# Issuing the later adaLN rows from ScalarE's queue in a one-core transformer layer

## The chip, the core and the metric

One core of a Trainium2 chip runs one transformer layer from HBM to HBM in one launch. The metric is the device time in microseconds of that launch. The engines are named as in the profile: PE is TensorE (matrix products), DVE is VectorE, ACT is ScalarE, POOL is GpSimd, and SP is the sync engine, which here issues transfers and nothing else. Every engine works through its own list of instructions in order; an instruction whose input is not there holds all that stand behind it on the same engine.

## The reference

SEQ is 256 tokens, D is 2048, the feed-forward width is 5632:

```python
ada = silu(c) @ w_ada + b_ada                     # 2048 -> 9 x 2048
sh1, sc1, g1, sh2, sc2, g2, sh3, sc3, g3 = split(ada, 9)
h = _swiglu(_modulate(x, sh1, sc1), ffn1_w_in, ffn1_w_out)
x = _layernorm(ALPHA * x + 0.5 * (1 + g1) * h, ln1_g, ln1_b)
h = _token_mixer(_modulate(x, sh2, sc2), w_in, ...)    # Fox attention and an mLSTM, side by side
x = _layernorm(ALPHA * x + (1 + g2) * h, ln2_g, ln2_b)
h = _swiglu(_modulate(x, sh3, sc3), ffn2_w_in, ffn2_w_out)
x = _layernorm(ALPHA * x + 0.5 * (1 + g3) * h, ln3_g, ln3_b)

def _modulate(x, shift, scale): return _layernorm(x) * (1 + scale) + shift
def _swiglu(h, w_in, w_out):
    gate, up = split(h @ w_in, 2)
    return (silu(gate) * up) @ w_out
```

All of it is float32. The vector `silu(c) @ w_ada` is the part that this case is about: one row vector times a matrix of 2048 x 18432, 151 MB, of which each number is used once.

## The kernel before

**Weights.** Each large product is made of three matrix products of rounded halves: a weight is split into `hi` (rounded to fp32r) and `lo = raw - hi`, and `mm3` multiplies hi by hi, hi by lo and lo by hi (lines L445 to L447; `mm2`, L450 and L451, is a form of it with two instructions). `load_w` brings a weight tile of 1 MB into one of three `raw` buffers (transfer issued by SP, L406), and `split` makes two halves of it: ScalarE casts `hi` (`S.copy`, L155) and VectorE subtracts `lo` (L156). There are six `hi` and six `lo` buffers. In most stages one half tile feeds twelve matmuls of 512 columns. Names: `raw_f1i9_11` is the raw tile of the first FFN's input weights, group 9, tile 11; `hi_f1i9_110` and `lo_f1i9_110` are its first half, `..._111` its second. `fv512` are columns of the mixer's input weights that make the Fox values; there a raw tile is cut in four, `hi_fv512_10` to `hi_fv512_13`.

**Ada rows.** VectorE computes `silu(c) @ w_ada` while TensorE multiplies weights. A *unit* is 1024 columns of `w_ada`; its 2048 input rows come as sixteen tiles of 128 x 1024, "rows" in this text, 512 KB each. `ask` takes the next row from the list `wanted`, takes one of two `araw` buffers, and issues its transfer (L192); `ada_acc` scales each of the 128 partitions by its element of `silu(c)` and adds it to the unit's accumulator (L168 for the first row, L170 for the others: `acc <- ar, csil, acc`). In `ada_rows` each accumulation is followed by the request for the next row, so one row is under way while another is used, and the row two later can only be issued when the accumulation of this one has ended. `ar3_0_14` is row 14 of unit 3_0. When a unit is complete, `pair_tail` or `gate_tail` split the sum and add it over the partitions on TensorE (`alo`, `bc`).

**What sets the order.** `AdaQueue` paces the rows: `pump(n)` and `half_step()` let about 1.1 to 1.3 rows through per raw weight tile, and `pinned()` places a row's work behind the newest weight cast; `need(n)` forces units to be complete ahead of their use. Within that, a scheduler that works from its own estimates puts the instructions of each engine in a fixed list when the kernel is built. The first rows, until about 220 us, are issued by GpSimd (L955); 224 later ones by `ask`. SP's list is thus a mixture of weight tiles (L406) and rows (L192).

Of the kernel before, what the change touches and what calls it, by code (L numbers as in the profile page):

```python
# [14 lines left out]
P = 128  # L15
# [17 lines left out]
def layer_kernel(  # L33
# [8 lines left out]
    V, S, G_, PE, SP = nc.vector, nc.scalar, nc.gpsimd, nc.tensor, nc.sync  # L42
# [143 lines left out]
    wanted, asked = [], []  # L186

    def ask():
        if wanted:
            shape, src, tag, k = wanted.pop(0)  # L190
            asked.append(ap.tile(shape, F32, tag="araw", bufs=2, name=f"ar{tag}_{k}"))
            SP.dma_start(asked[-1], src[k * P:(k + 1) * P])  # L192

    def ada_rows(acc):
        for k in range(KD):
            if not asked:
                ask()
            ada_acc(acc, asked.pop(0), k)
            ask()
            yield  # L200
# [1613 lines left out]
```

## Time and profile before

| | us |
|---|---|
| three runs | 1854.41, 1858.54, 1861.12 |
| median | 1858.54 |
| the profiled execution | 1855.95 |
| its span | 1854.2 |
| PE busy | 1820.5 |
| DVE busy | 1452.9 |
| ACT busy | 926.3 |

The granted TensorE clock of the profiled execution is 0.997 in the mean. Busy times are of the profiled execution; the three runs were timed apart from it. Matmul ends are modelled, so what TensorE loses is read from the starts of its matmuls and from its waits, not from its busy share. A row of a view of waits gives the engine and line that waited, what it waited for, the time in all, how often, and the longest. In rows by time the columns are start, duration, engine, line, operation, output and inputs, and in brackets the idle time ahead and what ended it; a row with x2 holds two or more instructions in a row, and its duration runs from the first's start to the last's end.

### The profile page before, as it was taken

How to read it: one execution, taken by the hardware profiler on the slowest of the kernel's cores; microseconds unless marked ns; L12 is line 12 of the kernel's file. 1: busy time of each engine (PE TensorE's matmuls, PEld its weight loads, DVE VectorE, ACT ScalarE, POOL GpSimd, SP SyncE). 2: the span in 40 equal slices, each digit the busy share in tenths (PEclk: the TensorE clock that was granted, in tenths of full speed). 3: DMA queues.
4: the chain of work that ended last, by engine and by line, in shares of the span. 5: the costliest groups of instructions: out<-in, count | busy, mean ns of one | idle time of the engine just before them, and what ended most of it. 6: DMA issues, size and time to landing. Idle time of an engine off the chain costs nothing.

```text
span 1854.2 us, 25052 instructions
## 1 busy us (share of the span) xinstructions
PE 1820.5 (98%) x9577; PEld 1599.3 (86%) x9577; DVE 1452.9 (78%) x1787; ACT 926.3 (50%) x1332; POOL 61.7 (3%) x92
## 2 busy tenths in 40 slices
PE   7999999999999999999999999999999999999997
PEld 4888888888888888699999887888889999988887
DVE  6889989877787787788889888787997766564655
ACT  3554455443554344755666645555465444554441
POOL 1211100000000000000000000000000000000000
PEclk9999999999999999999999999999999999999999
DMA  9989978988988898489979883998877876666663
GB/s 364 379 293 328 328 231 304 328 308 299 312 294 276 304 305 315 151 295 320 325 264 307 327 298 117 326 347 287 303 255 254 274 233 201 205 204 201 203 202 144
DMA packets 242927, 510.44 MB, mean 275 GB/s; under 512 B 10834, under 2 KB 52466, under 8 KB 241784
## 3 DMA queue, kind: packets, MB, share of 16 engines
q1 hardware_dynamic: 234696, 477.90, 74.7%
q0 software_dynamic: 8112, 30.95, 4.8%
q8 instruction: 75, 1.23, 0.3%
q14 instruction: 44, 0.36, 0.0%
HBM read 506.71 MB, written 2.10 MB: 274 GB/s over the span
## 4 chain that ended last, share of the span: by engine, by line
PE 56%; DVE 1%; issue 1%; ACT 0%; DMA 0%; POOL 0%; DVEq 0%; ACTq 0%; POOLq 0%; SPq 0%
PE gu_f L450 8%; PE o_f L446 4%; PE o_f L445 4%; PE o_f L447 4%; PE gu_f L451 4%; PE fh L446 4%; PE fh L447 4%; PE fh L445 4%; PE o_mx L445 1%; PE o_mx L446 1%; PE o_mx L447 1%; PE b_mv L445 1%; PE b_fv L445 1%; PE pr_m L445 1%; PE b_mv L446 1%; PE b_fv L446 1%
## 5 line engine op out<-in xcount | busy, mean ns | idle before, releaser
L170 DVE SCALAR_TENSOR_TENSOR acc<-ar,csil,acc 128x1024 f32<-128x1024 f32 (+1 forms) x167 | 211.7, 1269 | 65.8 <-DMA ar<-in_w_ada_dram 65.4
L450 PE MATMUL gu_f<-x_f,hi_f2i 128*128 128x512 f32 x640 | 210.0, 382 | 0.0
L451 PE MATMUL gu_f<-x_f,lo_f2i 128*128 128x256 f32 x640 | 174.5, 273 | 0.0
L156 DVE TENSOR_TENSOR lo_f2o<-raw_f2o,hi_f2o 128x1024 fp32r<-128x1024 f32 x86 | 105.2, 1224 | 86.7 <-ACT hi_f2o L155 86.6
L155 ACT CAST hi_s<-raw_s 128x1024 fp32r<-128x1024 f32 x96 | 99.1, 1047 | 117.4 <-PE s L447 64.8
L155 ACT CAST hi_f1o<-raw_f1o 128x1024 fp32r<-128x1024 f32 x86 | 88.4, 1047 | 120.6 <-PE o_f L447 63.3
L155 ACT CAST hi_f2o<-raw_f2o 128x1024 fp32r<-128x1024 f32 x86 | 90.1, 1047 | 115.6 <-PE o_f L447 107.0
L446 PE MATMUL s<-lo_s,x_f 128*128 128x512 f32 x384 | 146.2, 381 | 1.2 <-DVE lo_s L156 1.1
L445 PE MATMUL s<-hi_s,x_f 128*128 128x512 f32 x384 | 146.4, 383 | 0.2 <-ACT x_f L359 0.2
L447 PE MATMUL s<-hi_s,x_f 128*128 128x512 f32 x384 | 145.5, 379 | 0.0
L156 DVE TENSOR_TENSOR lo_f2i<-raw_f2i,hi_f2i 128x1024 fp32r<-128x1024 f32 x80 | 97.9, 1224 | 54.2 <-ACT hi_f2i L155 53.7
L450 PEld LDWEIGHTS gu_f<-x_f,hi_f2i 128*128 128x128 f32 x640 | 121.0, 189 | 16.8
L445 PE MATMUL o_f<-hi_f1o,hi 128*128 128x512 f32 x344 | 131.4, 382 | 3.1 <-DVE hT L1021 2.0
L447 PE MATMUL o_f<-hi_f1o,lo 128*128 128x512 f32 x344 | 131.0, 381 | 0.0
L446 PE MATMUL o_f<-lo_f1o,hi 128*128 128x512 f32 x344 | 131.0, 381 | 0.0
L155 ACT CAST hi_f1i<-raw_f1i 128x1024 fp32r<-128x1024 f32 x80 | 81.1, 1045 | 99.4 <-DMA raw_f1i<-in_ffn_w_in_dram 71.8
L170 DVE SCALAR_TENSOR_TENSOR gate<-ar,csil,gate 128x1024 f32<-128x1024 f32 (+1 forms) x94 | 117.5, 1251 | 16.3 <-DMA ar<-in_w_ada_dram 15.9
L156 DVE TENSOR_TENSOR lo_s<-raw_s,hi_s 128x1024 fp32r<-128x1024 f32 x96 | 115.9, 1220 | 14.8 <-ACT hi_s L155 14.8
L445 PE MATMUL o_f<-hi_f2o,hi 128*128 128x512 f32 x332 | 125.8, 379 | 0.0
L446 PE MATMUL o_f<-lo_f2o,hi 128*128 128x512 f32 x332 | 125.8, 379 | 0.0
L447 PE MATMUL o_f<-hi_f2o,lo 128*128 128x512 f32 x332 | 125.8, 379 | 0.0
L155 ACT CAST hi_fh<-raw_fh 128x1024 fp32r<-128x1024 f32 x80 | 82.4, 1048 | 81.3 <-DMA raw_fh<-in_ffn_w_in_dram 37.0
(447 smaller groups left out, 4830.7 us busy)
## 6 DMA issues: line engine op xcount, KB each, us to landing
ar<-in_w_ada_dram SPq DMA_DIRECT2D x230, 512.0 KB, 5.5
raw_s<-in_ffn_w_in_dram SPq DMA_DIRECT2D x47, 1024.0 KB, 7.6
raw_f1o<-in_ffn_w_out_dram SPq DMA_DIRECT2D x44, 1024.0 KB, 7.3
raw_f2o<-in_ffn_w_out_dram SPq DMA_DIRECT2D x44, 1024.0 KB, 5.0
raw_f1i<-in_ffn_w_in_dram SPq DMA_DIRECT2D x40, 1024.0 KB, 7.5
raw_fh<-in_ffn_w_in_dram SPq DMA_DIRECT2D x40, 1024.0 KB, 7.4
raw_f2i<-in_ffn_w_in_dram SPq DMA_DIRECT2D x40, 1024.0 KB, 5.8
ar<-in_w_ada_dram POOLq DMA_DIRECT2D x45, 512.0 KB, 6.3
```

What stands on the lines that cost most here:

```text
L155: S.copy(hi, src)
L156: return V.tensor_tensor(out=lo, in0=src, in1=hi.bitcast(F32), op=ALU.subtract)
L170: V.scalar_tensor_tensor(out=acc, in0=raw, scalar=csil[:, k:k + 1], in1=acc, op0=ALU.mult, op1=ALU.add)
L445: PE.matmul(o, ah, bh, start=start, stop=False)
L446: PE.matmul(o, ah, bl, start=False, stop=False)
L447: PE.matmul(o, al, bh, start=False, stop=stop)
L450: PE.matmul(o, ah, x.rearrange("p s (a n) -> p s n a", a=2), start=start, stop=False)
L451: PE.matmul(o[:, T:], al, woven(x[:, 0]), start=False, stop=stop)
```

## The change

The transfer of a later ada row is issued by ScalarE (`S` is `nc.scalar`) where the sync engine issued it:

```diff
@@ ask() @@
             shape, src, tag, k = wanted.pop(0)
             asked.append(ap.tile(shape, F32, tag="araw", bufs=2, name=f"ar{tag}_{k}"))
-            SP.dma_start(asked[-1], src[k * P:(k + 1) * P])
+            S.dma_start(asked[-1], src[k * P:(k + 1) * P])
```

The transfer itself, its buffers and its place in the program's text are the same. The lists that the scheduler makes are not: ScalarE's has the 224 row issues, SP's has them no more, and in some places VectorE's order is another one.

Place one is in the first FFN's input product, where unit 3_0 ends. ScalarE before (`hT` are copies of transposed activations):

```order
L155 CAST hi_f1i9_100_3748<-raw_f1i9_10_3746 128x1024
L155 CAST hi_f1i9_101_3767<-raw_f1i9_10_3746 128x1024
L986 COPY hT116_124<-th32_0_3651 128x2x128
L986 COPY hT117_125<-th32_0_3651 128x2x128
L986 COPY hT116_124<-th32_1_3652 128x2x128
L986 COPY hT117_125<-th32_1_3652 128x2x128
L155 CAST hi_f1i9_110_3788<-raw_f1i9_11_3786 128x1024
L155 CAST hi_f1i9_111_3804<-raw_f1i9_11_3786 128x1024
```

and now:

```order
L155 CAST hi_f1i9_100_3748<-raw_f1i9_10_3746 128x1024
L192 DMA ar3_0_14_3724<-in_w_ada_dram 128x2x512
L155 CAST hi_f1i9_101_3767<-raw_f1i9_10_3746 128x1024
L986 COPY hT116_124<-th32_0_3651 128x2x128
L986 COPY hT117_125<-th32_0_3651 128x2x128
L986 COPY hT116_124<-th32_1_3652 128x2x128
L986 COPY hT117_125<-th32_1_3652 128x2x128
L192 DMA ar3_0_15_3765<-in_w_ada_dram 128x2x512
L192 DMA ar3_1_0_3784<-in_w_ada_dram 128x2x512
L155 CAST hi_f1i9_110_3788<-raw_f1i9_11_3786 128x1024
```

Three row issues stand among the casts; `hi` 110 is behind the issue of `ar3_1_0`, which waits for the accumulation of row 14. VectorE at the same place, before:

```order
L170 SCALAR_TENSOR_TENSOR acc3_0_3291<-ar3_0_12_3666,csil_94,acc3_0_3291 128x1024
L170 SCALAR_TENSOR_TENSOR acc3_0_3291<-ar3_0_13_3703,csil_94,acc3_0_3291 128x1024
L156 TENSOR_TENSOR lo_f1i9_101_3768<-raw_f1i9_10_3746,hi_f1i9_101_3767 128x1024
L156 TENSOR_TENSOR lo_f1i9_110_3789<-raw_f1i9_11_3786,hi_f1i9_110_3788 128x1024
L170 SCALAR_TENSOR_TENSOR acc3_0_3291<-ar3_0_14_3724,csil_94,acc3_0_3291 128x1024
L170 SCALAR_TENSOR_TENSOR acc3_0_3291<-ar3_0_15_3765,csil_94,acc3_0_3291 128x1024
L156 TENSOR_TENSOR lo_f1i9_111_3805<-raw_f1i9_11_3786,hi_f1i9_111_3804 128x1024
```

and now:

```order
L170 SCALAR_TENSOR_TENSOR acc3_0_3291<-ar3_0_13_3703,csil_94,acc3_0_3291 128x1024
L156 TENSOR_TENSOR lo_f1i9_101_3768<-raw_f1i9_10_3746,hi_f1i9_101_3767 128x1024
L170 SCALAR_TENSOR_TENSOR acc3_0_3291<-ar3_0_14_3724,csil_94,acc3_0_3291 128x1024
L170 SCALAR_TENSOR_TENSOR acc3_0_3291<-ar3_0_15_3765,csil_94,acc3_0_3291 128x1024
L156 TENSOR_TENSOR lo_f1i9_110_3789<-raw_f1i9_11_3786,hi_f1i9_110_3788 128x1024
L156 TENSOR_TENSOR lo_f1i9_111_3805<-raw_f1i9_11_3786,hi_f1i9_111_3804 128x1024
```

The cast `lo` 110 moved behind the accumulations of rows 14 and 15.

Place two is in the mixer, at the Fox value columns. ScalarE before (`og` are the output gates):

```order
L1564 ACTIVATE og1_6576<-mo10_6364 128x256
L1564 ACTIVATE og2_6577<-mo11_6365 128x256
L1564 ACTIVATE og3_6578<-mo11_6365 128x256
L155 CAST hi_fv512_10_6693<-raw_fv512_1_6691 128x520
L155 CAST hi_fv512_11_6709<-raw_fv512_1_6691 128x520
```

and now:

```order
L192 DMA ar6_0_7_6564<-in_w_ada_dram 128x2x512
L192 DMA ar6_0_8_6654<-in_w_ada_dram 128x2x512
L1564 ACTIVATE og0_6575<-mo00_6362 128x256
L1564 ACTIVATE og1_6576<-mo00_6362 128x256
L1564 ACTIVATE og2_6577<-mo01_6363 128x256
L1564 ACTIVATE og3_6578<-mo01_6363 128x256
L1564 ACTIVATE og0_6575<-mo10_6364 128x256
L1564 ACTIVATE og1_6576<-mo10_6364 128x256
L1564 ACTIVATE og2_6577<-mo11_6365 128x256
L1564 ACTIVATE og3_6578<-mo11_6365 128x256
L192 DMA ar6_0_9_6673<-in_w_ada_dram 128x2x512
L155 CAST hi_fv512_10_6693<-raw_fv512_1_6691 128x520
```

Rows 7 and 8 stand ahead of the gates, and row 9 stands between them and `hi` 10. VectorE there, before:

```order
L156 TENSOR_TENSOR lo_fv512_10_6694<-raw_fv512_1_6691,hi_fv512_10_6693 128x520
L156 TENSOR_TENSOR lo_fv512_11_6710<-raw_fv512_1_6691,hi_fv512_11_6709 128x520
L170 SCALAR_TENSOR_TENSOR acc6_0_5908<-ar6_0_7_6564,csil_94,acc6_0_5908 128x1024
L156 TENSOR_TENSOR lo_fv512_12_6726<-raw_fv512_1_6691,hi_fv512_12_6725 128x520
L170 SCALAR_TENSOR_TENSOR acc6_0_5908<-ar6_0_8_6654,csil_94,acc6_0_5908 128x1024
```

and now:

```order
L170 SCALAR_TENSOR_TENSOR acc6_0_5908<-ar6_0_7_6564,csil_94,acc6_0_5908 128x1024
L1596 MEMSET u_0_1_7671 128x2x4
L170 SCALAR_TENSOR_TENSOR acc6_0_5908<-ar6_0_8_6654,csil_94,acc6_0_5908 128x1024
L156 TENSOR_TENSOR lo_fv512_10_6694<-raw_fv512_1_6691,hi_fv512_10_6693 128x520
L156 TENSOR_TENSOR lo_fv512_11_6710<-raw_fv512_1_6691,hi_fv512_11_6709 128x520
L156 TENSOR_TENSOR lo_fv512_12_6726<-raw_fv512_1_6691,hi_fv512_12_6725 128x520
```

The casts `lo` 10 and 11 moved behind the accumulations of rows 7 and 8.

## The prediction

> **What bounds the kernel now.** I read the page first, then the waits of TensorE and of the sync engine's queue, then the rows' own tile, and last the stretches in which a wait of TensorE ends.
>
> ```profile
> PE 1820.5 (98%) x9577; PEld 1599.3 (86%) x9577; DVE 1452.9 (78%) x1787; ACT 926.3 (50%) x1332; POOL 61.7 (3%) x92
> PE   7999999999999999999999999999999999999997
> ```
> ```profile
> PE o_f L445 <- DVE hT L1021: 2.0, 1, 2.0
> ...
> PE gu_f L446 <- DVE lo_f1i L156: 1.2, 2, 0.7
> ...
> PE bc L183 <- DVE alo L156: 0.4, 1, 0.4
> ```
> ```profile
> SPq L192 <- DVE acc L170: 233.3, 125, 7.0
> ...
> SPq L192 <- DMA ar<-in_w_ada_dram: 146.0, 90, 3.5
> ...
> SPq L192 <- DVE gate L170: 129.9, 64, 7.7
> ```
>
> TensorE is busy 98% of the span, every slice but the first and last at 90% or more. After the start-up its waits are a handful; those that end in a weight or row cast on VectorE are 1.2 + 0.4 us, and none ends in a weight transfer. So the 509 us (233.3 + 146.0 + 129.9) for which the sync engine stands at an ada row are nearly all beside TensorE's work: freeing it can return only what TensorE loses, a few us. Whatever delays a cast of VectorE beyond the lead it has on TensorE, however, lands on the end at once.
>
> **The change, part by part.**
>
> *Issues.* 224 row transfers leave the sync engine and go to ScalarE.
>
> ```profile
> L192 SPq DMA_DIRECT2D ar<-in_w_ada_dram x224: 327/367/500, 220.6 to 1499.1; - x112
> ...
> DMA to landing us min/median/max: 3.6/5.8/10.4
> ```
>
> 224 x 0.367 = 82 us of issue. ScalarE is busy 926.3 us; with this it would be 1008, or 54%. No ScalarE row shows such an issue, so I take the sync engine's; the nearest other case is the same operation issued from GpSimd, at twice that. Covered by ScalarE's idle time: 0. Issues that are not covered are in the second rival.
>
> *The wait moves too.* A row may be issued only when one of two buffers is free, that is when VectorE has accumulated the row two before. Until now the sync engine stood there; ScalarE is in order, so now everything behind the row in its list stands: weight hi casts, activations, gate scalings. A harmless case, in the mixer:
>
> ```profile
> 939.21 5.72 SPq L192 DMA_DIRECT2D ar<-in_w_ada_dram  x2
> ```
> ```profile
> 943.70 0.39 ACT L1582 ACTIVATE qs<-pr_fb 128x256 f32<-128x256 f32 x1 [1.57 <-PE pr_fb L447]
> 945.15 0.73 ACT L1505 ACTIVATE dm<-gb,nacol 128x256 f32<-128x256 f32 x2 [1.05 <-PE gb L1502]
> ```
>
> The second issue ends at 939.21 + 5.72 = 944.93. In the new order it stands ahead of `qs`, which so slips from 943.70 to 944.93, but the following `dm` starts 0.18 us late, because ScalarE was idle 1.05 us ahead of it. Over most of the kernel the cover is of this kind, or the lead of up to six hi/lo pairs over TensorE. I take 0 for all places but two, where the order of VectorE changes as well.
>
> *Place one, the tenth column group of the first FFN.* Before, VectorE made `lo` of tile 110 ahead of the last two rows of unit 3_0; now both rows come first. Below, in VectorE's order: casts 101 and 110 in one line, rows 14 and 15, cast 111; then the two issues of rows 14 and 15, and TensorE.
>
> ```profile
> 455.60 2.35 DVE L156 TENSOR_TENSOR lo_f1i<-raw_f1i,hi_f1i 128x1024 fp32r<-128x1024 f32 x2
> 458.79 1.28 DVE L170 SCALAR_TENSOR_TENSOR acc<-ar,csil,acc 128x1024 f32<-128x1024 f32 x1 [0.84 <-DMA ar<-in_w_ada_dram]
> 460.90 1.28 DVE L170 SCALAR_TENSOR_TENSOR acc<-ar,csil,acc 128x1024 f32<-128x1024 f32 x1 [0.83 <-DMA ar<-in_w_ada_dram]
> 462.11 1.22 DVE L156 TENSOR_TENSOR lo_f1i<-raw_f1i,hi_f1i 128x1024 fp32r<-128x1024 f32 x1
> ```
> ```profile
> 454.39 1.69 SPq L192 DMA_DIRECT2D ar<-in_w_ada_dram  x2
> ```
> ```profile
> 461.68 0.38 PE L445 MATMUL gu_f<-hi_f1i,x_f 128*128 128x512 f32 x1
> ...
> 462.33 0.38 PE L445 MATMUL gu_f<-hi_f1i,x_f 128*128 128x512 f32 x1
> 463.38 0.48 PE L446 MATMUL gu_f<-lo_f1i,x_f 128*128 128x512 f32 x1 [0.67 <-DVE lo_f1i L156]
> 463.70 0.38 PE L447 MATMUL gu_f<-hi_f1i,x_f 128*128 128x512 f32 x1
> ```
>
> Both rows waited for their landing, so they don't come earlier by themselves: row 15 ends at 460.90 + 1.28 = 462.18, and cast 110 follows, to about 463.4 instead of 457.95. TensorE starts a matmul each 0.216 us (461.68 to 462.33 are three), twelve to a tile, 2.59 us; it would have wanted `lo` 111 at 462.54, so it wants `lo` 110 at 462.54 - 2.59 = 459.95. It stands 3.4 us. Cast 111 ends 1.1 us behind 110, within the tile. The 0.84 us (463.38 - 462.54) lost there today go: +2.5 us. Ends: if both rows land at the shortest 3.6 us instead of their 4.4 (458.79 less 454.39) and 5.2 (460.90 less 455.71, the second issue's start: 454.39 + 1.69 - 0.37), cast 110 is ready some 1.5 sooner, +1.0. If ScalarE issues row 15 late, which it must (cast `hi` 101 and row 14 stand ahead of it and wait), by one VectorE operation, +3.7.
>
> *Place two, the fox value columns of the mixer.* ScalarE now has rows 7 and 8, eight gate activations and row 9 ahead of the hi cast of tile 10, and row 9 waits for row 7's accumulation; VectorE has rows 7 and 8 ahead of `lo` 10, which it did at 810.54 before.
>
> ```profile
> 808.94 1.69 SPq L192 DMA_DIRECT2D ar<-in_w_ada_dram  x2
> ```
> ```profile
> 809.88 1.68 ACT L155 CAST hi_fv<-raw_fv 128x520 fp32r<-128x520 f32 x3
> ```
> ```profile
> 810.54 1.31 DVE L156 TENSOR_TENSOR lo_fv<-raw_fv,hi_fv 128x520 fp32r<-128x520 f32 x2
> 812.89 1.28 DVE L170 SCALAR_TENSOR_TENSOR acc<-ar,csil,acc 128x1024 f32<-128x1024 f32 x1 [1.04 <-DMA ar<-in_w_ada_dram]
> ...
> 815.80 1.28 DVE L170 SCALAR_TENSOR_TENSOR acc<-ar,csil,acc 128x1024 f32<-128x1024 f32 x1 [1.01 <-DMA ar<-in_w_ada_dram]
> ```
> ```profile
> 814.94 0.28 PE L446 MATMUL b_fv<-lo_fv,x_mx 128*128 128x256 f32 x1
> ```
>
> Row 7 is accumulated by 814.17, so row 9 goes out and the hi cast ends near 815.2 (809.88 to 810.5 before): not yet the last thing. Row 8 was issued at 810.26 (808.94 + 1.69 - 0.37), waited for its landing, and ends at 817.08; `lo` 10 then takes some 0.65 (half of 1.31), to 817.7. TensorE wants it at 814.94: 2.75 us. The following tiles come each 0.6 to 0.7 on VectorE and are used one per 1.43 us, so the loss stands once: +2.75. Ends: row 8 landing in 3.6 instead of 5.5 us gives +0.8; each of the two rows in the loop held back by one tile of 1.43 us on ScalarE gives +5.6.
>
> *The clock behind a wait.* Today's longest wait of TensorE has a tail:
>
> ```profile
> 521.21 0.38 PE L447 MATMUL o_f<-hi_f1o,lo 128*128 128x512 f32 x1
> 523.55 0.48 PE L445 MATMUL o_f<-hi_f1o,hi 128*128 128x512 f32 x1 [1.97 <-DVE hT L1021]
> ...
> 524.74 0.53 PE L447 MATMUL o_f<-hi_f1o,lo 128*128 128x512 f32 x1
> ...
> 528.05 0.48 PE L446 MATMUL o_f<-lo_f1o,hi 128*128 128x512 f32 x1
> ```
> ```profile
> 520.00:530.00 10.00, 8.03 (x30) 6.39 (x29) 8.04 (x8) 7.80 (x12) 0.00 (x0) 0.83 0.71 259
> ```
>
> Nine matmuls need 524.74 to 528.05, 3.3 us instead of 1.9, and the granted clock of those ten us is 0.83. Such a tail costs about 1.5 us. The 0.84 us wait at 463 has none, so a tail hangs on a wait of some 2 us. Two waits of 2.75 and 3.4 us may have 0 to 2 tails; I take one, +1.5.
>
> *The weights alone.* With no row ahead of them they can only go out earlier. Where TensorE waited for a weight cast today, 429 and 462 us, it was VectorE's order that held the cast. I take half of the 1.2 us, -0.6; the ends are 0 and all three waits quoted at first, -3.6.
>
> Sum: 2.5 + 2.75 + 1.5 - 0.6 = +6.2 us. The profiled execution took 1855.95 (span 1854.2), which gives 1862.2; it is 2.6 below the median of the runs, 1858.54, and on that the same +6.2 gives 1864.7. I forecast 1865. What a measurement of this kernel can tell from no change is about 0.3%, 5.6 us, so the forecast lies just on the slower side.
>
> The Trainium skill, page "DMA: Bandwidth & Descriptors", section "Issuing engines are not separate DMA queues", says that transfers from ScalarE, the sync engine and GpSimd run on the same 16 DMA engines and interleave, so that spreading the issues saves only sequencer time. By that rule the second queue brings no bandwidth; the rows here agree so far as the sync engine's 509 us of standing cost TensorE next to nothing. By it alone the sum would be 0, and the time 1858.5; that it leaves the waits of the issuing engine out is why I stay with +6.2.
>
> **The rivals.**
>
> *Rows land sooner, nothing changes.* Today a row is behind the weight tile issued ahead of it in the same queue: 10.4 us at the longest against 3.6 at the shortest. On a queue of their own most may land near the short end. Then both places shrink to their lower ends, 1.0 + 0.8, without tails and with the -0.6: +1.2, 1859.7. For it: both places hang on landings (0.84, 0.83, 1.04, 1.01 us waited). Against: the bytes are the same, and the DMA engines are 0.89 busy in both stretches:
>
> ```profile
> 400.00:470.00 70.00, 68.33 (x319) 58.88 (x318) 51.97 (x49) 28.15 (x39) 0.54 (x1) 1.00 0.89 311
> ...
> 790.00:1000.00 210.00, 209.91 (x1628) 202.44 (x1627) 180.21 (x285) 123.50 (x231) 5.48 (x9) 1.00 0.89 302
> ```
>
> The same page, section "Queues, rings and completion order", has each DMA engine take turns between the queues for which it has work, packet by packet. By that rule a row would share with a weight tile rather than stand behind it, which is this rival; no run here shows it yet.
>
> *ScalarE becomes what bounds.* If the standing holds rows back as well, the row loop itself slows, and the same loss comes in other stretches with small leads. Both places at their upper ends (3.7 + 5.6), both tails (3.0) and three more such places at the mean of the two central prices (3 x 2.6): +20, 1879. It decides when a hi cast slips further than its lead. For it: VectorE is 180 of 210 us busy in the mixer, with little to catch up in. Against: ScalarE has 40% of that stretch free.
>
> *Faster.* The weights come early enough to remove all three quoted waits and the tail at 524: -3.6 - 1.5 = -5.1, 1853.4. For it: the sync engine's waits. Against: those three end in VectorE, and it has no fewer operations.
>
> **How the numbers follow.** My forecast has 0.52, rows landing sooner 0.28, ScalarE as the bound 0.12, faster 0.08. The forecast's own range, from one place at its lower end without a tail (1858.54 + 2.9) to both upper ends with one tail (+10.2), is 1861 to 1869. Mostly slower by more than 0.3%, but about a tenth of it within; so slower 0.57, same 0.36, faster 0.07. The range that holds 8 in 10 reaches to the second rival's 1879, and below to 1856, past the first.
>
> **What would show it.** Issues of the rows under ScalarE, near 0.37 us each; the sync engine's waits at L192 gone but for a few. TensorE's waits should have a row for `gu_f` from the `lo_f1i` cast of some 3 us, near 460 us, and one for `b_fv` from `lo_fv` of 2 to 3 us near 815, with a granted clock below 1 behind one of them. If the landing median falls from 5.8 to below 5 us and those two rows are absent, the first rival is right. If the span grows by more than 15 us, TensorE's waits would name hi and lo casts in several stretches, and ScalarE's idle time would be put down to its own queue. If TensorE's total is unchanged with both places on time, my reading of VectorE's order was wrong.

## The result and the profile after

| | before | after |
|---|---|---|
| median of the runs, us | 1856.92 (4 runs, 1854.41 to 1861.12) | 1879.3 (4 runs, 1873.35 to 1880.76) |
| ratio, with its 95% interval | | 1.0112 [1.0087, 1.0137] |
| the profiled execution, us | 1855.95 | 1873.35 |
| its span, us | 1854.2 | 1871.3 |
| its mean granted clock | 0.997 | 0.996 |

The change made the kernel 1.1% slower: 22.4 us by the medians, 17.1 us between the two profiled spans, the one after being that of the shortest of its four runs. What follows accounts for those 17; the other 5 have no trace. No engine has much more to do. The lines of the profile page after on busy time, the queues and the chain that ended last, and then the chain before:

```profile
PE 1826.1 (98%) x9577; PEld 1602.3 (86%) x9577; DVE 1454.1 (78%) x1787; ACT 926.1 (49%) x1332; POOL 62.0 (3%) x92
...
q1 hardware_dynamic: 186056, 360.45, 55.7%
q10 hardware_dynamic: 48640, 117.45, 18.4%
...
PE 48%; DVE 5%; DMA 3%; issue 2%; ACT 1%; POOL 0%; ACTq 0%; DVEq 0%; POOLq 0%
```
```profile
PE 56%; DVE 1%; issue 1%; ACT 0%; DMA 0%; POOL 0%; DVEq 0%; ACTq 0%; POOLq 0%; SPq 0%
```

VectorE was busy 1454.1 us against 1452.9 and ScalarE 926.1 against 926.3, and PE's busy time grew by 5.6 us only. The rows, 117 MB, now have a queue of their own. TensorE's share of the chain fell from 56 to 48%, VectorE's grew from 1 to 5% and that of DMA from 0 to 3%. The row loop, by its transfers (the view of one tile; duration is minimum, median and maximum in ns):

```profile
L192 ACTq DMA_DIRECT2D ar<-in_w_ada_dram x224: 334/374/2828, 222.1 to 1516.0; - x112
...
DMA to landing us min/median/max: 3.6/6.0/10.4
```

The issues are on ScalarE, 0.374 us each, none of the sync engine's waits names L192 any more, and rows do not land sooner: the median is 6.0 us where it was 5.8 (both with the first 51 rows; on the pages, 5.7 for the 224 moved rows against 5.5). Nor does ScalarE hold the rows back: of 222 moved rows all but 5 went out within half a us of their buffer coming free; from the sync engine it was all but 3. The new waits are ScalarE's and, behind them, VectorE's and TensorE's (views of waits: time in all, times, longest):

```profile
ACT hi_f1o L155 <- DVE acc L170: 51.2, 23, 5.2
ACT hi_f1i L155 <- DVE acc L170: 27.2, 10, 4.7
...
ACT hi_f1i L155 <- DVE gate L170: 18.6, 9, 3.2
```
```profile
DVE acc L170 <- DMA ar<-in_w_ada_dram: 78.1, 54, 5.0
...
DVE lo_f1i L156 <- ACT hi_f1i L155: 16.4, 15, 3.0
...
DVE lo_f1o L156 <- ACT hi_f1o L155: 11.9, 12, 4.1
```
```profile
PE o_f L445 <- DVE hT L1021: 3.0, 1, 3.0
PE gu_f L446 <- DVE lo_f1i L156: 2.9, 3, 1.3
...
PE o_f L446 <- DVE lo_f1o L156: 2.2, 2, 1.9
PE b_fv L445 <- ACT og L1564: 2.2, 1, 2.2
...
PE pr_fb L447 <- DVE lo_fb L156: 1.6, 1, 1.6
```

A hi cast does not read an accumulation. "`hi_f1o` waits for `acc`" means that a row's issue stood ahead of the cast in ScalarE's list and waited for its buffer. All such waits of ScalarE, summed over the view's rows that name `acc` or `gate` of the row loop, come to 208 us in 94 waits; before, they were 26 us in 9, all of them the `ahi` cast that really reads a sum. Of VectorE the same rows before:

```profile
DVE acc L170 <- DMA ar<-in_w_ada_dram: 65.4, 60, 2.8
...
DVE lo_f1i L156 <- ACT hi_f1i L155: 18.5, 10, 4.0
DVE lo_f1o L156 <- ACT hi_f1o L155: 16.1, 10, 3.9
```

VectorE's wait for rows grew from 65.4 to 78.1 us at `acc`, and the longest from 2.8 to 5.0. Its waits for hi casts did not grow in the first FFN, and over the whole kernel they come to 218 us against 232. So the link that one expects, a held cast that VectorE then waits for, is not where most of VectorE's new waiting is. TensorE has small new waits in many places, none over 3 us.

Where the time went, by the start of the same matmul in the two traces (what TensorE falls behind in each stretch, us; the stretches are on the clock of the changed kernel, here and below):

| kernel | to 220 | 220 to 460 | 460 to 700 | 700 to 800 | 800 to 1000 | later | sum |
|---|---|---|---|---|---|---|---|
| after | +2.0 | +2.3 | +1.1 | +4.6 | +7.0 | 0.0 | 17.0 |

The first column is start-up scatter from ahead of the first moved row. Each kernel has one trace, and the later columns scatter too: e4 below, whose median shows no loss, gains 5.0 us on the trace of before between 460 and 700, mostly because the wait at 521 us and the slow clock behind it are missing there. A single place of a us or two is therefore not proven by the table. The largest single place is at 700 to 722 us, the end of the first FFN. ScalarE's casts there before (rows by time), in pairs, one pair per raw tile, these two as soon as the weight has landed:

```profile
700.46 1.99 ACT L155 CAST hi_f1o<-raw_f1o 128x1024 fp32r<-128x1024 f32 x2 [5.50 <-DMA raw_f1o<-in_ffn_w_out_dram]
...
707.04 2.00 ACT L155 CAST hi_f1o<-raw_f1o 128x1024 fp32r<-128x1024 f32 x2 [1.43 <-DMA raw_f1o<-in_ffn_w_out_dram]
```

And after, with VectorE and TensorE at the same place:

```profile
697.70 1.05 ACT L155 CAST hi_f1o<-raw_f1o 128x1024 fp32r<-128x1024 f32 x1 [1.42 <-DVE acc L170]
703.44 0.38 ACTq L192 DMA_DIRECT2D ar<-in_w_ada_dram  x1
703.91 1.05 ACT L155 CAST hi_f1o<-raw_f1o 128x1024 fp32r<-128x1024 f32 x1 [5.17 <-DVE acc L170]
...
709.20 1.04 ACT L155 CAST hi_f1o<-raw_f1o 128x1024 fp32r<-128x1024 f32 x1 [1.89 <-DVE acc L170]
```
```profile
702.12 1.29 DVE L170 SCALAR_TENSOR_TENSOR acc<-ar,csil,acc 128x1024 f32<-128x1024 f32 x1 [3.81 <-DMA ar<-in_w_ada_dram]
703.32 1.22 DVE L156 TENSOR_TENSOR lo_f1o<-raw_f1o,hi_f1o 128x1024 fp32r<-128x1024 f32 x1
...
705.65 1.22 DVE L156 TENSOR_TENSOR lo_f1o<-raw_f1o,hi_f1o 128x1024 fp32r<-128x1024 f32 x1
...
710.27 1.23 DVE L156 TENSOR_TENSOR lo_f1o<-raw_f1o,hi_f1o 128x1024 fp32r<-128x1024 f32 x1 [0.45 <-ACT hi_f1o L155]
...
715.39 0.69 DVE L556 SCALAR_TENSOR_TENSOR res<-res,o_f 128x512 f32<-128x512 f32 x1
715.99 1.22 DVE L156 TENSOR_TENSOR lo_f1o<-raw_f1o,hi_f1o 128x1024 fp32r<-128x1024 f32 x1
```
```profile
717.27 0.48 PE L446 MATMUL o_f<-lo_f1o,hi 128*128 128x512 f32 x1 [1.94 <-DVE lo_f1o L156]
```

VectorE waits 3.81 us for a row, which was issued at 694.76, at once when its buffer was free, and took 7.4 us to be there. The issue of the row two later waits for VectorE's accumulation, and the cast of a weight that landed at 692.1 stands 5.17 us behind that issue. The correction that needs this cast (705.65) did not have to wait for it, since VectorE was as late itself; the one at 710.27 waited 0.45 us for the cast at 709.20, which had stood behind the next issue. The store of finished `lo` tiles that carried TensorE over VectorE's epilogue (its operations at L554 to L562, up to 715.39) is gone: the six corrections ahead of the epilogue were finished 7.7 to 3.5 us before TensorE used them, and are now 3.2 to 0.1 us. TensorE stands 1.94 us. So here the waits for rows and ScalarE's standing act together, and the trace does not part them. Where ScalarE's standing reaches TensorE directly is in the mixer:

```profile
818.87 2.18 ACTq L192 DMA_DIRECT2D ar<-in_w_ada_dram  x2
```
```profile
ACT og L1564 <- DVE acc L170: 6.0, 1, 6.0
```
```profile
821.95 0.39 PE L445 MATMUL b_fv<-hi_fv,x_mx 128*128 128x264 f32 x1 [2.19 <-ACT og L1564]
```

The gate activations stand 6.0 us behind two row issues, and TensorE waits 2.19 us for them. Two more of its waits end in ScalarE's work behind an issue: 0.66 us for a hi cast at 464, and 1.0 us for `yF` at 846. At 715 the granted clock falls behind the wait (a stretch of five us; x counts instructions, and the column behind POOL is the granted clock):

```profile
719.00:724.00 5.00, 5.00 (x18) 4.17 (x18) 5.00 (x5) 1.99 (x2) 0.00 (x0) 0.74 0.74 255
```

### The profile page after: what moved, and what is told of

Its sections match the earlier page's. It is cut to its first block, busy times and chain, and to the rows that moved or that the text cites. A ratio compares the mean times of both kernels' runs of the same rounds, so it can differ in the third digit from the quotient of the medians.

```text
span 1871.3 us, 25048 instructions
## 1 busy us (share of the span) xinstructions
PE 1826.1 (98%) x9577; PEld 1602.3 (86%) x9577; DVE 1454.1 (78%) x1787; ACT 926.1 (49%) x1332; POOL 62.0 (3%) x92
## 4 chain that ended last, share of the span: by engine, by line
PE 48%; DVE 5%; DMA 3%; issue 2%; ACT 1%; POOL 0%; ACTq 0%; DVEq 0%; POOLq 0%
PE gu_f L450 7%; PE o_f L447 4%; PE o_f L446 4%; PE o_f L445 4%; PE gu_f L451 4%; PE fh L445 4%; PE fh L447 4%; PE fh L446 4%; DMA ar<-in_w_ada_dram 2%; PE o_mx L447 1%; PE o_mx L445 1%; PE o_mx L446 1%; DVE acc L170 1%; PE ge L793 1%; DVE gate L170 1%
## 5 line engine op out<-in xcount | busy, mean ns | idle before, releaser
L170 DVE SCALAR_TENSOR_TENSOR acc<-ar,csil,acc 128x1024 f32<-128x1024 f32 (+1 forms) x167 | 211.7, 1269 | 78.7 <-DMA ar<-in_w_ada_dram 78.1
L446 PE MATMUL gu_f<-lo_f1i,x_f 128*128 128x512 f32 x320 | 121.6, 380 | 2.9 <-DVE lo_f1i L156 2.9
```

The source lines that it names most:

```text
L170: V.scalar_tensor_tensor(out=acc, in0=raw, scalar=csil[:, k:k + 1], in1=acc, op0=ALU.mult, op1=ALU.add)
L446: PE.matmul(o, ah, bl, start=False, stop=False)
```

## The experiments

Three theories ran through the expectations: that ScalarE standing at issues delays casts and corrections (A), that two queues share the DMA engines and so weights or rows land later (B), and that the issues themselves take ScalarE's time (C). Two joined them: that VectorE's new order is the cause (D), and that weights which no longer stand behind rows run ahead of them (E). A moved issue makes the scheduler rearrange all lists, so several runs fix the lists by ordering edges. Ratios are to runs of the kernel before on the same chip.

| run | rows issued by | order of the lists | median us | ratio [95%] |
|---|---|---|---|---|
| after | ScalarE | its own | 1879.3 | 1.0112 [1.0087, 1.0137] |
| e1_pool | GpSimd | its own | 1882.16 | 1.0132 [1.0107, 1.0157] |
| e2_act_ffn1 | ScalarE for units 2 and 3 | its own | 1869.48 | 1.0063 [1.0040, 1.0086] |
| e3_act_rest | ScalarE for units 5, 6 and 8 | its own | 1868.08 | 1.0059 [1.0041, 1.0078] |
| e4_issue_only | SP, and 224 tiny transfers by ScalarE | its own | 1855.37 | 0.9987 [0.9974, 0.9999] |
| e5_act_oldorder | ScalarE | VectorE's rows and corrections as before | 1872.58 | 1.0082 [1.0064, 1.0101] |
| e6_sp_neworder | SP | VectorE's rows and corrections as after | 1873.66 | 1.0093 [1.0072, 1.0113] |
| e7_pool_oldorder | GpSimd | VectorE's rows and corrections as before | 1876.15 | 1.0108 [1.0089, 1.0127] |
| f1_act_lists | ScalarE | all lists as before | 1875.14 | 1.0096 [1.0079, 1.0113] |
| f3_act_hold | ScalarE | as before, weights held | 1879.66 | 1.0123 [1.0103, 1.0143] |
| f4_pool_hold | GpSimd | as before, weights held | 1881.97 | 1.0134 [1.0114, 1.0154] |
| g1_act_unread | ScalarE | as before, rows not read | 2079.54 | 1.1192 [1.1168, 1.1215] |
| g2_sp_unread | SP | as before, rows not read | 1851.04 | 0.9971 [0.9960, 0.9981] |

### e1_pool: another engine that has time

```diff
-            SP.dma_start(asked[-1], src[k * P:(k + 1) * P])
+            G_.dma_start(asked[-1], src[k * P:(k + 1) * P])
```

> The 224 rows are issued by GpSimd instead of ScalarE: still a queue other than the weights', but the engine that stands at a row has almost nothing behind it. Theory A (standing: an in-order ScalarE that waits for a row's buffer holds hi casts back, and VectorE's order with them): no loss, 1854 to 1861 us. Theory B (two queues share the DMA engines, and weights or rows land later): a loss like the change's, 1870 to 1880. Theory C (the issues themselves take ScalarE's time): no loss.

It lost as much, 1.0132, where GpSimd is 3% busy in the kernel before. Theory A had expected no loss here, and B this one. So ScalarE as the issuer is not needed for a loss of this size. VectorE's order is a new one here too, which e7 takes away. TensorE's waits are again for corrections:

```profile
PE gu_f L446 <- DVE lo_f1i L156: 4.5, 4, 2.4
PE o_f L446 <- DVE lo_f1o L156: 4.0, 4, 1.7
PE bc L183 <- DVE alo L156: 4.0, 1, 4.0
```

### e2_act_ffn1 and e3_act_rest: the two halves

```diff
-            SP.dma_start(asked[-1], src[k * P:(k + 1) * P])
+            (S if tag[0] in "23" else SP).dma_start(asked[-1], src[k * P:(k + 1) * P])   # e2
+            (SP if tag[0] in "23" else S).dma_start(asked[-1], src[k * P:(k + 1) * P])   # e3
```

> Only the rows of units 2 and 3, which are used in the first FFN (220 to 705 us), are issued by ScalarE, the rest by the sync engine. In the changed kernel's trace TensorE falls back 7 us between 230 and 730 us and 7 us between 800 and 970. Theory A: about half of the loss, 1862 to 1868, and TensorE's lag stops growing at 730 us. Theory B: the same share by rows (112 of 224). Theory C: 82/2 us of issues, spread in proportion, without steps.

> The other half: only the rows of units 5, 6 and 8 (mixer and second FFN) by ScalarE. Theory A: the other half of the loss, 1862 to 1869, all of it between 800 and 970 us and nothing after 1160, where the leads of hi and lo over TensorE are 8 us and more. Theory B: a loss after 1160 us as well, where half of these rows are.

Each half costs about half, +0.63% and +0.59%, which add up to the whole. It is not one unlucky place. The stretches differ: e2 falls behind by 5.2 us between 220 and 700 and by 1.4 from 700 to 1000; e3 by 8.7 between 800 and 1000 and by a further 3.3 later, near 1065 and 1113, where theory A had expected all of it between 800 and 970; 4.7 us of e3 are start-up scatter. The wait that I had placed at 815 us is there in e3, again ended by ScalarE's activations `og`, 2.9 us long.

### e4_issue_only: the issues without the waits

The rows stay with SP, and ScalarE issues 224 extra transfers of 4 bytes, each reading the hi cast behind which it stands, so that none of them waits for another engine.

```diff
+        if due and len(hi.shape) == 3:
+            due.pop()
             ...
+            S.dma_start(dots[j % P:j % P + 1, j // P:j // P + 1], hi[0:1, 0, 0:1].bitcast(F32))
```

> Rows stay with the sync engine; ScalarE issues 224 further transfers of 4 bytes each, every one behind a hi cast of its own that it reads, so nothing on another engine is waited for. This keeps the 224 issues of about 0.37 us on ScalarE and takes the standing away. Theory A: 1856 to 1860. Theory C: most of the loss, 1870 and more.

0.9987: nothing lost. The largest group of these issues:

```profile
L163 ACTq DMA_DIRECT2D dots<-hi_f1i x47: 569/570/588, 294.2 to 501.2; - x47
```

At 0.57 us they cost ScalarE 224 x 0.57 = 128 us, more than the 84 us (224 x 0.374) of the change. Theory C is out: what hurts is not the issuing.

### e5, e6 and e7: whose order is it

```diff
-            V.tensor_scalar_mul(acc, raw, csil[:, k:k + 1])
+            return V.tensor_scalar_mul(acc, raw, csil[:, k:k + 1])
             ...
+    # each accumulation and each lo goes behind the one ahead of it in DVE_ORDER (an ordering edge, no wait)
```

> The changed kernel (rows issued by ScalarE) with VectorE's order of weight casts (lo) and row accumulations fixed to that of the kernel before, by ordering edges that add no wait. GpSimd lost as much as ScalarE, so the standing of ScalarE alone can't be it. Theory D (VectorE's new order, which puts accumulations ahead of casts although the rows land no sooner): most of the loss goes, 1857 to 1863. Theory A (ScalarE's standing): the loss stays, 1870 to 1880. Theory B (two queues): stays.

> The kernel before (rows issued by the sync engine) with VectorE's order of weight casts and accumulations fixed to that of the changed kernel. Theory D: the loss comes without any change of queue, 1868 to 1880, with waits of TensorE near 465, 715 and 815 us. Theories A and B: no loss, 1855 to 1861.

> Rows issued by GpSimd with VectorE's order fixed to that of the kernel before: own queue, no standing of ScalarE, old order. Theory D: 1855 to 1860, the whole loss of 24 us gone. Theory B (two queues share the DMA engines): 1870 and more. If the weights alone on their queue bring anything by themselves, it is seen here: below 1855.

All three lost, 1.0082, 1.0093 and 1.0108. Theory D had expected e5 and e7 to lose little or nothing, theories A and B the same of e6. e6 shows that VectorE's new order is enough by itself: with the rows still on the sync engine, and ScalarE's waits for sums about as short as before (30 us in 11), it falls behind by 7.4 us between 460 and 700, and TensorE waits for corrections again:

```profile
PE gu_f L528 <- DVE lo_f1i L238: 4.8, 3, 3.3
PE b_fv L528 <- DVE lo_fv L238: 2.9, 1, 2.9
```

e5 and e7 show that it is not needed. In e5 some 130 entries of VectorE's list still stood at another place than before, which left room for D; in e7 it was 27. The next runs closed it.

### f1, f3 and f4: every list as before

```diff
+    for text in ORDERS.values():            # the lists of all five engines, as the kernel before had them
+        line = [seen[k] for k in ...]
+        for a, b in zip(line, line[1:]):
+            behind(b, a, False)             # an ordering edge, no wait
+    for b, a in HOLDS:                      # f3 and f4 only
+        behind(seen[b], seen[a], True)      # a weight transfer waits for the sum for which SP stood before
```

> The rows are issued by ScalarE, and the lists of all five engines are fixed to those of the kernel before, entry for entry; only the 224 issues change from the sync engine's list to ScalarE's. Theory D (the new lists are the cause): 1856 to 1861. Theory A (ScalarE's standing) and theory E (with the rows gone from its list, the sync engine no longer stands at a row, so weight tiles go out ahead of rows that would have gone first, and a row behind a fresh weight tile lands about 1.5 us later: 6.3 to 6.9 us against 4.7 to 5.2 in the traces so far): 1867 to 1878.

> As the run with ScalarE and all lists of before, and besides each weight transfer of the sync engine waits for the row accumulation for which the sync engine stood ahead of it before, so the weights are held as they were, while the rows go out from ScalarE. Theory E: the loss goes, 1856 to 1862. Theory A: the loss stays, 1867 and more. Theory B (two queues at all): stays.

> The same hold with the rows issued by GpSimd, which has nothing behind them that matters. GpSimd with the old order and weights alone took 1876. Theory E: 1857 to 1863, a little over the run with ScalarE because GpSimd issues a row 0.3 us later and takes 0.72 us for it. Theory B: 1870 and more.

With all lists identical and only the 224 issues moved, f1 is at 1.0096. So the move loses nearly 1% without any new list, and e6 loses as much by VectorE's list alone. In the kernel after both are there and the loss is 1.12%: the two do not add up, and what share each has in it is open. Holding the weights as before changes nothing for the better (1.0123 and 1.0134), though SP then stands some 250 us at weights for sums: theory E is out. In f1, ScalarE's waits for sums come to 182 us in 83, and TensorE's new waits are these:

```profile
PE o_f L454 <- DVE hT L1030: 3.8, 1, 3.8
...
PE o_f L455 <- DVE lo_f1o L165: 2.1, 1, 2.1
PE pr_m L456 <- DVE lo_m L165: 2.0, 2, 1.8
```

GpSimd's loss looks different. In e7, ScalarE's casts of weights hardly stand for a sum; what stands is the cast that reads the finished one:

```profile
ACT ahi L237 <- DVE acc L251: 39.6, 8, 11.2
```
```profile
L273 POOL DMA_DIRECT2D ar<-in_w_ada_dram x224: 528/722/752, 220.6 to 1524.6; - x112
```

GpSimd takes 0.722 us for an issue, and starts it 0.3 us after the buffer is free, where SP and ScalarE start after 0.03. With two buffers this would slow the loop where it runs at its fastest: in the two units whose rows are used from 575 to 704 us before, an accumulation starts every 3.73 us in e7 (first to last row, mean of the two units), against 3.32 before, 3.29 in e4, 3.42 after and 3.46 in f1. The sums then end later, and e7 loses 10.0 us between 700 and 800. That the slow issue is the cause is argued, not shown: no run changed it alone, and the loop is slow in e6 too, 3.59, where SP issues the rows.

### g1 and g2: rows that nobody reads

All lists and transfers as in f1 (g1) and as before (g2), but from the second row of each unit on the accumulation reads its own accumulator, so that the shift, scale and gate vectors are not computed from those rows.

```diff
-            V.scalar_tensor_tensor(out=acc, in0=raw, scalar=csil[:, k:k + 1], in1=acc,
+            V.scalar_tensor_tensor(out=acc, in0=acc if later else raw, scalar=csil[:, k:k + 1], in1=acc,
```

> Rows issued by ScalarE, every engine's list as before, all transfers of the same size and in the same order, but from the second row of each vector on VectorE's accumulation reads its own accumulator instead of the row (so the shift, scale and gate vectors are not computed from those rows). VectorE then waits for no such row, and ScalarE, at an issue, no longer stands for an accumulation, only for the landing of the row two before in the same buffer. If the loss is the coupling of rows, ScalarE and VectorE (an accumulation waits for a row, a hi cast behind an issue waits for an accumulation, a lo correction for that cast), it is gone: 1850 to 1858 us, within 3 us of g2_sp_unread. If two queues on the same DMA engines are the cause by themselves (weights late for TensorE), the transfers are all still there: 1868 to 1878 us. If ScalarE standing at an issue for the landing alone is enough, in between, with ScalarE waiting for DMA ahead of issues and TensorE waiting for lo tiles.

> The control for g1_act_unread: rows issued by the sync engine as before, every engine's list as before, the accumulations likewise not reading the rows. By every theory it is not slower than before: 1848 to 1857 us. What it gains on before is what VectorE's waits for rows cost there; the coupling theory expects little, up to 8 us, since TensorE waited there only some us; the theory of the DMA engines expects none.

Neither theory expected g1: 224 us slower. It is not a clean test, since it made a new wait. A row's issue started within 0.2 us of the landing of the row just before it in 77% of cases (5% in f1), so rows went one at a time, and ScalarE stood at the issues:

```profile
ACT hi_f1o L164 <- DMA ar<-in_w_ada_dram: 98.6, 24, 6.7
ACT hi_f1i L164 <- DMA ar<-in_w_ada_dram: 79.8, 23, 7.0
...
ACT hi_fh L164 <- DMA ar<-in_w_ada_dram: 52.1, 13, 5.9
```

All waits of this kind come to 389 us in 105. In its control the sync engine stands for landings, though mostly for that of the row two before (46% of the issues followed it within 0.2 us, and 3% the row just before):

```profile
SPq L201 <- DMA ar<-in_w_ada_dram: 194.2, 108, 5.4
```

There 194 us of standing for landings cost nothing; the kernel is even 0.3% faster, 0.9971 [0.9960, 0.9981]. This agrees with the view that who stands is what matters: work that feeds TensorE is behind ScalarE's wait, and only further transfers behind SP's. It does not prove it, since the two runs differ in the wait too. The 4 us by which g2 beats before may be what VectorE's waits for rows cost TensorE even in the kernel before. By the starts of the matmuls g2 gains 7.6 us between 220 and 700, but e4, which reads all rows, gains 4.6 us there as well.

Whether two queues by themselves delay anything (B) was not separated: every run with the rows on a second queue had either ScalarE standing or GpSimd's slower issue, and all of them lost, as B expects. Against B stand e6, which lost with one queue, and the landings. The weight transfers between 230 and 720 us whose landing is recorded, 42 to 56 of some 88, took 7.15 us in the mean before, and 6.8 to 7.2 us in after and in each of e1, e5, e7, f1, f3 and f4. The rows issued between 220 and 760 us whose arrival shows, by a recorded landing or by the wait that it ended, took 5.6 us before and 5.4 to 5.8 us in those runs. Their medians over all moved rows are a little longer, 5.7 to 6.0 us against 5.5, mainly by the rows behind 1000 us, where TensorE loses next to nothing. A third `araw` buffer, which would loosen the row loop, was not tried. No run that computed the whole layer beat the kernel before by more than 0.3%.

## Why the prediction was right, and where it was off

**Right: the direction, and the first half of the mechanism.** The time is slower by more than 0.3%, and the reason given, that ScalarE stands at a row's issue until VectorE has accumulated the row two before, is what its waits show. f1 shows that the move of the issues is enough for the loss with all lists as before. How the standing reaches TensorE is seen directly in three waits only (3.9 us together); the rest of that path is argued. The issues at zero cost: confirmed by e4 with 1.5 times their time.

**Off: the size**, +22.4 us by the medians against +6.2. 1879.3 is at the very top of the range 1856 to 1879 that was to hold 8 in 10, and far outside the forecast's own 1861 to 1869. Term by term:

- *Place one, +2.5.* TensorE's waits near 464 us are there: 0.66 and 1.22 by the trace, against 0.84 before, and it falls behind by 1.5 us. Inside the bounds of 1.0 to 3.7. The first of the two waits ends in a hi cast, ahead of which ScalarE had stood 4.1 us at an issue.
- *Place two, +2.75.* TensorE falls behind by 2.8 us at 800 to 820. The size was right by luck, since the last link was another: the wait is ended by ScalarE's activations `og`, which stand 6.0 us behind a row's issue (rows above), and not by `lo_fv`. The cast that I had named did stand:

```profile
813.59 1.68 ACT L155 CAST hi_fv<-raw_fv 128x520 fp32r<-128x520 f32 x3 [3.75 <-DVE acc L170]
```

- *One clock tail, +1.5.* There is a new one behind the wait at 715 us, 1.6 us, which is neither of the two places that I had named, and that behind 521 us in the trace before is now behind 530.
- *The weights alone, -0.6.* No gain shows: of the two waits on which the term rested, TensorE is even over the one at 429 us and loses a further 1.5 us at 464; at the third, that at 521, it loses 1.0 more.
- *ScalarE's standing elsewhere, 0.* This is the term that was mis-sized. I had taken it that the other casts have enough lead, from one case in the mixer and the six hi/lo pairs. The places missed cost +1.6 at 374, +1.0 at 530, +4.5 at 704 to 722, +1.2 at 846, +1.9 at 951 and +1.1 at 970: 11.3 us together, the new clock tail among them. What covered VectorE's epilogues before, a store of finished halves, was used up at 715, as the leads there show. That ScalarE's 182 us more of standing did this is not shown: of these places only the one at 846 ends in ScalarE's work behind an issue, and at 374 and 715 VectorE had stood 3.5 and 3.8 us for a row.
- *The lists.* I took VectorE's new order as free apart from the two places. e6 puts it at +0.9% by itself, so taking it as free was wrong, though f1 shows that the loss does not need it.

**The rivals.** "Rows land sooner" is refuted by the landing median of 6.0 us. The rule of the Trainium skill, page "DMA: Bandwidth & Descriptors", section "Queues, rings and completion order", on which it leaned, that DMA engines take turns between queues, would not have been enough: sharing did not shorten a row's way. The rule of the Trainium skill, on the same page in section "Issuing engines are not separate DMA queues", that issuing from several engines saves only the time on the sequencer agrees with e4, where 128 us of further issues cost nothing. It does not give the time here: f1 lost 0.96% with nothing moved but the issues. "ScalarE becomes what bounds", 1879, had the time right, in part by luck: it took both places at their upper ends and three more, where the two came to 1.5 and 2.8 us and some six more made up the rest. Its condition, rows held back, hardly shows: they went out when their buffers were free, and the loop at 575 to 704 us went from 3.32 to 3.42 us a row. I gave it 0.12, and ScalarE is only half the story: e1 and e7 lose as much with ScalarE out of it.

## What to carry to other kernels

An issue cost ScalarE little time here, but it brought its buffer wait into ScalarE's list, and everything behind it waited too. Ask not only how busy the new issuer is but what stands behind the issue and whom that feeds; SP, which does nothing else here, stood for some 509 us beside a TensorE that was 98% busy. That is not enough to make a move safe: GpSimd, with next to nothing behind its issues, lost as much. A moved issue also makes new lists, and these alone cost 0.9% here, so fix the lists by ordering edges before comparing issuers. Where TensorE is 98% busy and another engine 78% in a fixed list, treat the leads read from one trace as a shared store: price the standing over a stage, not place by place.

## What was not expected of the hardware

- An issue by GpSimd took 0.72 us and began 0.3 us after its buffer was free; by ScalarE and SP it took 0.37 us and began after 0.03 us. A 4-byte transfer took ScalarE longer to issue (0.57 us) than a 512 KB row (0.37 us).
- A wait of TensorE of 1.94 us was followed by five us at a granted clock of 0.74, in which 18 matmuls ran; at the same place before it was 25 in five us:

```profile
706.00:711.00 5.00, 5.00 (x25) 4.38 (x24) 5.00 (x8) 2.00 (x2) 0.00 (x0) 1.00 0.98 338
```

- Rows on their own queue landed no sooner: 5.7 us in the median by ScalarE and 5.8 by GpSimd, against 5.5 in one queue with the weights. What had been issued just before them mattered more: rows issued within 2.5 us of a weight tile took 6.7 us in the mean both before and after (38 and 53 rows with a recorded landing), and those issued more than 4.5 us behind one 4.8 and 4.5 us.
